# Attention of a Hymba-style step, regrouped: one narrow group of TensorE work per unit, with transposes two groups behind their scores

## The chip, the core and the metric

The kernel runs on one core of a Trainium2 chip. The metric is the device time of one execution in microseconds (us), the median of three runs. TensorE (PE) multiplies, VectorE (DVE), ScalarE (ACT) and GpSimd (POOL) do elementwise work, and SyncE (SP) issues the large loads.

## What is computed

One layer for 320 tokens (256 of a new stream, 64 of a running one), with `D_MODEL` 2048, 16 query heads and 2 key heads of 64, and an FFN of 8192. The reference, cut to what matters here:

```python
h = rmsnorm(x, ln_g); z = h @ w_in          # q 1024, k 128, v 128, u 1024, v 1024
q, k = rmsnorm(q, q_g), rmsnorm(k, k_g)     # per head
def sink_attention(q, k, v, bias, sinks):   # chunk of 64, own chunk and the 2 before it
    s = einsum(q, k) * HEAD_DIM ** -0.5 + bias
    m = maximum(max(s), sink)
    p = exp(s - m)
    return einsum(p / (sum(p) + exp(sink - m)), v)
a = gelu(zs); u, v = a[:1024], rmsnorm(a[1024:], g)
s_o = u * (w_s @ v + b_s)                   # 8 groups of channels, chunks of 128 positions
x = x + concat(rmsnorm(attn_o), rmsnorm(s_o)) @ w_out
y = x + square(relu(rmsnorm(x) @ w_up)) @ w_down
```

## The kernel before

Activations lie transposed: channels on partitions, 320 tokens along the free axis. Every dense product takes 256 columns of a weight at a time. A load (`w_raw`, 512 KB) brings 4 blocks of 128 rows; `halves` splits it into a high part (`w_hi`, ACT, L108) and the rest (`w_lo`, DVE, L109), and three matmuls high x high, high x low, low x high make up one product of float32 quality. Such a matmul (128x320 out, L133) is called a **wide** here, and one load a **step**: 24 wides. A product over 2048 rows has 4 steps, 96 wides. `w_hi` and `w_lo` have 3 buffers each, so a step's halves are written when the step three before it has been multiplied.

The wides run on in this order, counted from the first as W0: keys, values and q0 together up to W192, q1 to W288, q2 to W384, q3 to W480, four products for the SGU's `v` to W864, four for its `u` to W1248, `w_out` to W2016 (its attention half first), and then the FFN to W8160.

Everything else on PE is **narrow** float32 work between wides: `norm_q` (L311, sums of squares of q's heads), scores (`s_ps`, L385), transposes of the probabilities (L423), values (`o_ps`, L429), and for the SGU sums of rows (`rstd_rows`, L156), transposes (L485) and the spatial matmuls (L493). A **unit** of attention is a chunk of 64 queries with one key head; there are ten, `unit // 2` the chunk and `unit % 2` the head. Chunks 2 to 4 have 192 keys in two parts of 96, so two transposes each (`pt0`, `pt1`). Its softmax is spread over DVE (L394 to L404, L411, L412), ACT (L405, L409) and POOL (L413).

PSUM holds two accumulators (`acc`), one `s_ps`, and two buffers (`misc`) that all other narrow work shares. Each engine takes its instructions in the order of its own list. A scheduler lays these lists out when the kernel is built; `tc.issue_after(x)` puts what follows behind instruction x, and `between_pieces={n: ...}` places narrow work behind step n of a product. Attention (`attend`), the SGU's transposes and its spatial matmuls have no such place before; the scheduler spreads them among the wides of the `v` and the `u` products. `gelu2` (L452 to L460) reads a finished accumulator: `z` (DVE), a square (ACT), `gc` (DVE, then POOL), tanh (ACT), and the result (DVE).

Of the kernel before, what the change touches and what calls it, by code (L numbers as in the profile page):

```python
# [30 lines left out]
def hymba_step_kernel(ctx: ExitStack, tc: tile.TileContext, i, o):  # L31
# [63 lines left out]

    loads, between, steps, narrow = [], [], [], []

# [16 lines left out]

    def products(w, k0, nk, c0, ps, rh, rl, deep=None, between_pieces={}):

        wv = w.rearrange("(kt p) n -> p kt n", p=P)
        behind = None  # L120
        steps.clear()
        for a in range(0, nk, 4):
            raw = (deep or wp).tile([P, 4, 256], F32, name="w_raw", tag="w_raw")
            hi, lo = w_tiles()
            load(raw, wv[:, k0 + a:k0 + a + 4, c0:c0 + 256])
            high, low = halves(raw, hi, lo)
            tail = isinstance(ps, list) and a + 4 == nk
            for k, g in [(k, g) for g in range(2) for k in range(4)] if tail else [(k, g) for k in range(4) for g in range(2)]:
                kk = a + k
                for x, (w_, r_) in enumerate(((hi, rh), (hi, rl), (lo, rh))):  # L130
                    out = ps[g][:, 0:T] if isinstance(ps, list) else ps[:, g, 0:T]
                    with tc.issue_after(behind) if behind else nullcontext():
# [31 lines left out]
    def rstd(acc, mean, eps, out):  # L164
# [4 lines left out]
        nc.scalar.activation(out=hi, in_=acc, func=AF.Copy)  # L169
        nc.vector.tensor_tensor(out=lo, in0=acc, in1=hi.bitcast(F32), op=ALU.subtract)  # L170
        ps = misc()
# [83 lines left out]

    kzv = blk("kzv", [P, 1664])
    kz = kzv[:, 0:896].rearrange("p (h k) -> p h k", h=2)
# [69 lines left out]

    q1_ps = product(w_in, 0, KT, 256, xh, xl, between_pieces={0: lambda: rstd(ssq, mean_dm, EPS, rx)})

# [30 lines left out]
    q2_sq = evict_q(2, q2_ps)  # L360
    q3_ps = product(w_in, 0, KT, 768, xh, xl, between_pieces={0: lambda: norm_q(2, q2_sq)})
    norm_q(3, evict_q(3, q3_ps))


# [9 lines left out]

    def attend(unit):

        blk_, kv = unit // 2, unit % 2
        q0, k0, nk, b0, parts = blocks[blk_]
        js = slice(2 * kv, 2 * kv + 2)
        s_ps = ps_sc.tile([P, 2, 512], F32, name="s_ps", tag="s_ps")  # L380
        for j in range(2):
            a = 2 * (2 * kv + j)
            for p in range(2):
                hs = slice(p * HD, (p + 1) * HD)
                nc.tensor.matmul(out=s_ps[:, p, j * nk:(j + 1) * nk],  # L385
                                 lhsT=qT[hs, blk_, a:a + 2].rearrange("p a t -> p (a t)"),
                                 rhs=kz[hs, kv, k0:k0 + nk], start=True, stop=True)
        s = at.tile([P, 2, 2, 192], F32, name="s", tag="s", bufs=2)
        if nk < P:
# [17 lines left out]
        for p in range(2):  # L407
            for j in range(2):
# [5 lines left out]
                                in1=den[:, :, :, None].to_broadcast([P, 2, 2, nk]), op=ALU.mult)  # L414
        pts = []
        for x in range(len(parts)):
            pts.append(at.tile([P, 512], F32, name=f"pt{x}", tag=f"pt{x}", bufs=1))
        for x in reversed(range(len(parts))):
            n, c = parts[x][1], sum(n_ for _, n_ in parts[:x])
            pt_ps = misc()  # L420
            for p in range(2):
                for j in range(2):
                    nc.tensor.transpose(out=pt_ps[0:n, (2 * p + j) * P:(2 * p + j + 1) * P], in_=s[:, p, j, c:c + n],  # L423
                                        identity=ident)
            nc.vector.tensor_copy(out=pts[x][0:n], in_=pt_ps[0:n])
        o_ps = misc()
        for x, (pt, (v, n)) in enumerate(zip(pts, parts)):
            for p in range(2):
                nc.tensor.matmul(out=o_ps[p * HD:(p + 1) * HD, 0:256], lhsT=v[0:n, kv],  # L429
                                 rhs=pt[0:n, p * 256:(p + 1) * 256],  # L430
                                 start=(x == 0), stop=(x == len(parts) - 1))
# [11 lines left out]
    todo = list(range(10))
    after_q = [narrow[-1]]

    def attend_next(n):
        for _ in range(n):
            with tc.issue_after(after_q.pop()) if after_q else nullcontext():
                attend(todo.pop(0))

# [26 lines left out]
    rv = rstd_rows(acc_v, inv_1k, 4 * EPS)  # L477
    vnat = blk("vnat", [P, 2, 1024])
    vnat_s = at.tile([P, 1024], F32, name="vnat_s", bufs=1)
    nc.gpsimd.memset(vnat_s[HD:P], 0.0)  # L480
    for t, (t0, n) in enumerate(TT):
        for h in range(2):
            vps = misc()
            for a in range(4):
                nc.tensor.transpose(out=vps[0:n, a * P:(a + 1) * P], in_=gv[:, 4 * h + a, t0:t0 + n], identity=ident)  # L485
            dst = vnat[:, t] if t < 2 else vnat_s[0:HD]
            nc.scalar.activation(out=dst[:, h * 512:(h + 1) * 512], in_=vps[0:n], func=AF.Copy, scale=rv[0:n, t:t + 1])
    nc.gpsimd.dma_start(out=o["sgu_v"], in_=vnat_s[0:HD])
    for g in range(8):
        sp_ps = misc()  # L490
        cs = slice(g * P, (g + 1) * P)
        for b in range(2):
            nc.tensor.matmul(out=sp_ps[:, b * P:(b + 1) * P], lhsT=vnat[:, b, cs], rhs=wsT[:, g], start=True, stop=True)  # L493
        nc.tensor.matmul(out=sp_ps[:, 256:T], lhsT=vnat_s[:, cs], rhs=wsT[:, g, 0:HD], start=True, stop=True)
        nc.vector.tensor_tensor(out=gv[:, g, 0:256].rearrange("p (b i) -> p b i", b=2),
                                in0=sp_ps[:, 0:256].rearrange("p (b i) -> p b i", b=2),
                                in1=sgb[:, g, None, :].to_broadcast([P, 2, P]), op=ALU.add)
        nc.vector.tensor_tensor(out=gv[:, g, 256:T], in0=sp_ps[:, 256:T], in1=sgb[:, g, 0:HD], op=ALU.add)

    acc_s = sums("acc_s")  # L500
    rs_a, rm_a = [], rstd_b("rm_a")
    u_pieces = {3: {0: lambda: rs_a.append(rstd_rows(acc_a, inv_1k, EPS)), 2: lambda: spread(rs_a[0], rm_a)}}
    SH = SL = None
    for g in range(4):
        u_ps = product(w_in, 0, KT, 1280 + g * 256, xh, xl, between_pieces=u_pieces.get(g, {}))
        if g == 0:
            acc_a = sums_rows("acc_a")
            AH, AL = blk("AH", [P, 8, T], F32R), blk("AL", [P, 8, T], F32R)
            SH, SL = blk("SH", [P, 8, T], F32R), blk("SL", [P, 8, T], F32R)
        for x in range(2):  # L510
# [6 lines left out]
        gu = sm.tile([P, 2, T], F32, name="gu", tag="w2", bufs=4)  # L517
        gelu2(u_ps, gu)
        sp = gv[:, 2 * g:2 * g + 2]
        nc.vector.scalar_tensor_tensor(out=sp, in0=sp, scalar=0.5, in1=gu, op0=ALU.mult, op1=ALU.mult)  # L520
        for a in range(2 * g, 2 * g + 2):
            add_square(acc_s, gv[:, a], a == 0)
# [117 lines left out]
```

## Time and profile before

| what | value |
|---|---|
| median of 3 runs | 1257.11 us (1255.76 to 1257.68) |
| profiled execution, its time | 1254.9 us |
| its span in the trace | 1253.1 us |
| PE busy | 1245.4 us, 99% of the span |
| DVE, ACT, POOL busy | 658.8, 490.8, 97.0 us |
| granted clock of PE | 1.00 in the whole span |

The span is what the trace covers of the profiled execution, so 1.8 us of that execution lie outside it. The profiled execution is 2.2 us below the median. PE has some matmul in flight nearly all the time, and the 8160 wides are most of it. What a change of the narrow work does shows in where wides are interrupted and for how long.

### The profile page before, as it was taken

To read this page: it belongs to the slowest core of one execution; us is meant where nothing else is said; L and a number is where in the kernel's file an instruction comes from. 1 tells how busy PE (TensorE), PEld (TensorE's weight loads), DVE (VectorE), ACT (ScalarE), POOL (GpSimd) and SP (SyncE) were. 2 spreads that over 40 slices of the span, in tenths; PEclk is the share of its full clock that TensorE was granted. 3 is DMA by queue.
4 is the path that set the end of the run, shared out by engine and by line. 5 is a ranking of instruction groups with operands and counts; after the bars stand their busy time and mean duration, and the time that the engine had idled before them with its cause. 6 is when DMAs were issued, how large, how long until landed. Compare 5 with 4: busy or idle time off the path is not lost.

```text
span 1253.1 us, 20226 instructions
## 1 busy us (share of the span) xinstructions
PE 1245.4 (99%) x8519; PEld 1231.4 (98%) x8519; DVE 658.8 (53%) x767; ACT 490.8 (39%) x638; POOL 97.0 (8%) x97
## 2 busy tenths in 40 slices
PE   9999999999999999999999999999999999999998
PEld 8998899999999999999999999999999999999998
DVE  7848867776874443444444433444444444444443
ACT  7335556524544433323334333343333333443221
POOL 1223353301310000000000000000000000000000
PEclk9999999999999999999999999999999999999999
DMA  8743334644454444445454444445444444544550
GB/s 272 210 144 101 102 102 126 207 147 152 151 152 152 151 151 149 146 147 150 150 151 152 151 152 150 147 148 149 151 149 152 151 152 152 149 153 158 168 166 32
DMA packets 186555, 187.78 MB, mean 150 GB/s; under 512 B 6592, under 2 KB 185984, under 8 KB 186464
## 3 DMA queue, kind: packets, MB, share of 16 engines
q1 hardware_dynamic: 185824, 185.43, 47.7%
q8 instruction: 66, 1.08, 0.4%
q0 software_dynamic: 496, 1.03, 0.3%
q14 instruction: 25, 0.20, 0.0%
q10 hardware_dynamic: 144, 0.03, 0.0%
HBM read 182.91 MB, written 3.32 MB: 149 GB/s over the span
## 4 chain that ended last, share of the span: by engine, by line
PE 96%; DMA 2%; SPq 1%; ACT 0%; DVE 0%; issue 0%; ACTq 0%
PE acc L133 91%; PE misc L133 1%; DMA w_raw<-in_w_in 1%; PE misc L429 1%; PE s_ps L385 1%; DMA b_dram<-b_row 1%; PE misc L423 1%; SPq L103 1%; PE q_ps L237 0%; PE acc L237 0%; PE misc L311 0%; DMA w_first<-in_w_in 0%; ACT w_hi L108 0%; PE misc L493 0%; PE misc L485 0%; DVE w_lo L109 0%
## 5 line engine op out<-in xcount | busy, mean ns | idle before, releaser
L109 DVE TENSOR_TENSOR w_lo<-w_raw,w_hi 128x1024 fp32r<-128x1024 f32 x332 | 413.3, 1245 | 439.8 <-ACT w_hi L108 430.9
L108 ACT ACTIVATE w_hi<-w_raw 128x1024 fp32r<-128x1024 f32 x332 | 351.8, 1060 | 704.6 <-PE acc L133 675.0
L133 PE MATMUL acc<-H2H,w_hi 128*128 128x320 f32 x1024 | 316.4, 309 | 0.0
L133 PE MATMUL acc<-H2L,w_hi 128*128 128x320 f32 x1024 | 316.4, 309 | 0.0
L133 PE MATMUL acc<-H2H,w_lo 128*128 128x320 f32 x1024 | 316.4, 309 | 0.0
L133 PE MATMUL acc<-FH,w_hi 128*128 128x320 f32 x992 | 306.5, 309 | 0.0
L133 PE MATMUL acc<-FL,w_hi 128*128 128x320 f32 x992 | 306.5, 309 | 0.0
L133 PE MATMUL acc<-FH,w_lo 128*128 128x320 f32 x992 | 306.5, 309 | 0.0
L133 PEld LDWEIGHTS acc<-H2H,w_lo 128*128 128x128 f32 x1024 | 192.3, 188 | 0.0
L133 PEld LDWEIGHTS acc<-H2H,w_hi 128*128 128x128 f32 x1024 | 192.3, 188 | 0.0
L133 PEld LDWEIGHTS acc<-H2L,w_hi 128*128 128x128 f32 x1024 | 192.3, 188 | 0.0
L133 PEld LDWEIGHTS acc<-FH,w_hi 128*128 128x128 f32 x992 | 186.2, 188 | 0.0
L133 PEld LDWEIGHTS acc<-FL,w_hi 128*128 128x128 f32 x992 | 186.2, 188 | 0.0
L133 PEld LDWEIGHTS acc<-FH,w_lo 128*128 128x128 f32 x992 | 186.2, 188 | 0.0
L133 PE MATMUL acc<-XH,w_hi 128*128 128x320 f32 x352 | 110.5, 314 | 0.4 <-ACT ksq L334 0.4
L133 PE MATMUL acc<-XL,w_hi 128*128 128x320 f32 x352 | 110.2, 313 | 0.0
L133 PE MATMUL acc<-XH,w_lo 128*128 128x320 f32 x352 | 109.7, 312 | 0.0
L133 PEld LDWEIGHTS acc<-XH,w_hi 128*128 128x128 f32 x352 | 66.2, 188 | 2.2 <-issue 1.4
L133 PEld LDWEIGHTS acc<-XL,w_hi 128*128 128x128 f32 x352 | 66.2, 188 | 1.5 <-issue 1.4
L133 PEld LDWEIGHTS acc<-XH,w_lo 128*128 128x128 f32 x352 | 66.1, 188 | 1.0 <-issue 0.8
L557 DVE SCALAR_TENSOR_TENSOR tf<-acc,r 128x640 f32<-128x640 f32 x32 | 26.4, 825 | 41.9 <-PE acc L133 41.8
L571 DVE TENSOR_TENSOR xT<-xT,acc 128x640 f32<-128x640 f32 x31 | 25.5, 821 | 41.8 <-PE acc L133 41.8
(198 smaller groups left out, 1056.5 us busy)
## 6 DMA issues: line engine op xcount, KB each, us to landing
w_raw<-in_w_up SPq DMA_DIRECT2D x128, 512.0 KB
w_raw<-in_w_down SPq DMA_DIRECT2D x128, 512.0 KB
w_raw<-in_w_in SPq DMA_DIRECT2D x44, 512.0 KB
w_raw<-in_w_out SPq DMA_DIRECT2D x32, 512.0 KB
w_first<-in_w_in SPq DMA_DIRECT2D x15, 256.0 KB
out_yT<-xT SPq DMA_DIRECT2D x7, 320.0 KB
xT<-in_xT SPq DMA_DIRECT2D x8, 160.0 KB
xT<-in_xT SPq DMA_DIRECT2D x4, 320.0 KB
```

What stands on the lines that cost most here:

```text
L103: loads.append(nc.sync.dma_start(out=o_, in_=i_))
L108: return (pin(nc.scalar.activation(out=hi, in_=raw, func=AF.Copy)).ins, pin(nc.vector.tensor_tensor(out=lo, in0=raw, in1=hi.bitcast(F32), ...
L109: pin(nc.vector.tensor_tensor(out=lo, in0=raw, in1=hi.bitcast(F32), op=ALU.subtract)).ins)
L133: mm = nc.tensor.matmul(out=out, lhsT=w_[:, k, g * P:(g + 1) * P], rhs=r_(kk), start=(kk == 0 and x == 0), stop=(kk == nk - 1 and x == 2))
L385: nc.tensor.matmul(out=s_ps[:, p, j * nk:(j + 1) * nk], lhsT=qT[hs, blk_, a:a + 2].rearrange("p a t -> p (a t)"), rhs=kz[hs, kv, k0:k0 + n ...
L423: nc.tensor.transpose(out=pt_ps[0:n, (2 * p + j) * P:(2 * p + j + 1) * P], in_=s[:, p, j, c:c + n], identity=ident)
L429: nc.tensor.matmul(out=o_ps[p * HD:(p + 1) * HD, 0:256], lhsT=v[0:n, kv], rhs=pt[0:n, p * 256:(p + 1) * 256], start=(x == 0), stop=(x == l ...
L557: nc.vector.scalar_tensor_tensor(out=t, in0=ps[:, :, 0:T], scalar=0.0, in1=r2[:, None, :].to_broadcast([P, 2, T]), op0=ALU.max, op1=ALU.mult)
L571: nc.vector.tensor_tensor(out=xT[:, a:a + n], in0=xT[:, a:a + n], in1=p, op=ALU.add)
```

## The change

- Units are taken head by head (all chunks of key head 0, then of 1). `attend(i)` is now one group: the values of unit i-3, the scores of unit i, the transposes of unit i-2. Group i stands at W432 + 48 i, that is behind steps 1 and 3 of q3 and of the `v` products, and the last three groups in the first two `u` products.
- Probabilities `s` have three buffers. The transposed probabilities lie at the ends of `kzv` and of a tile `room` that also holds `vnat`.
- `norm_q(2)` moves from W408 to W432, `norm_q(3)` from W512 to W528. The SGU's transposes stand at W984, W1008 and W1032, its spatial matmuls by twos from W1056 on.
- A pin (`behind`) at the end of a product now holds for the wides of the next one (`carry`).
- x's norm: DVE takes the split of `acc` (L170) ahead of `w_lo` of q1's third step.
- `SH` is written one `u` product later, and its rest `SL` (8 DVE passes) moves into the attention half of `w_out`.

```diff
@@ products @@
-        behind = None
+        behind = carry.pop() if carry else None
...
-            high, low = halves(raw, hi, lo)
+            with tc.issue_after(halves_behind[a // 4]()) if a // 4 in halves_behind else nullcontext():
+                high, low = halves(raw, hi, lo)
...
                     behind = narrow[-1]
+                if a + 4 == nk:
+                    carry.append(behind)
@@ rstd, q1 @@
-        nc.vector.tensor_tensor(out=lo, in0=acc, in1=hi.bitcast(F32), op=ALU.subtract)
+        rests.append(nc.vector.tensor_tensor(out=lo, in0=acc, in1=hi.bitcast(F32), op=ALU.subtract).ins)
...
-    q1_ps = product(w_in, 0, KT, 256, xh, xl, between_pieces={0: lambda: rstd(ssq, mean_dm, EPS, rx)})
+    q1_ps = product(w_in, 0, KT, 256, xh, xl, between_pieces={0: lambda: rstd(ssq, mean_dm, EPS, rx)},
+                    halves_behind={2: lambda: rests[-1]})
@@ attention @@
-    q3_ps = product(w_in, 0, KT, 768, xh, xl, between_pieces={0: lambda: norm_q(2, q2_sq)})
-    norm_q(3, evict_q(3, q3_ps))
...
+    units = [(b, kv) for kv in range(2) for b in range(5)]
+    probs, turned = {}, {}
+    room = blk("vnat", [P, 2560])
+    vnat = room[:, 0:2048].rearrange("p (t c) -> p t c", t=2)
+    pts = [kzv[:, 1664:2176], room[:, 2048:2560]]
...
-        s = at.tile([P, 2, 2, 192], F32, name="s", tag="s", bufs=2)
+        s = at.tile([P, 2, 2, 192], F32, name="s", tag="s", bufs=3)
...
+    def attend(i):
+
+        for stage, u in ((values_of, i - 3), (scores, i), (turn, i - 2)):
+            if 0 <= u < 10:
+                with tc.issue_after(narrow[-1]):
+                    stage(u)
+
+    q3_ps = product(w_in, 0, KT, 768, xh, xl,
+                    between_pieces={1: lambda: (norm_q(2, q2_sq), attend(0)), 3: lambda: attend(1)})
+    q3_sq = evict_q(3, q3_ps)
@@ SGU @@
-        attend_next((4, 3, 3, 0)[g])
-        v_ps = product(w_in, 0, KT, 2304 + g * 256, xh, xl)
+        v_ps = product(w_in, 0, KT, 2304 + g * 256, xh, xl, between_pieces={
+            1: lambda: (norm_q(3, q3_sq) if g == 0 else None, attend(2 * g + 2)), 3: lambda: attend(2 * g + 3)})
...
+        0: {1: lambda: attend(10), 3: last_values},
+        1: {0: lambda: by_rows((0, 0), (1, 0)), 1: lambda: (attend(12), by_rows((2, 0), (0, 1))),
+            2: lambda: by_rows((1, 1), (2, 1)), 3: lambda: spatial(0, 1)},
+        2: {0: lambda: spatial(2, 3), 1: lambda: spatial(4, 5), 2: lambda: spatial(6, 7)},
...
-            split(gv[:, a], g_os[:, a:a + 1], SH[:, a], SL[:, a])
...
+            if half == 0:
+                with tc.issue_after(steps[0][1]):
+                    nc.vector.scalar_tensor_tensor(out=SL[:, g], in0=gv[:, g], scalar=g_os[:, g:g + 1],
+                                                   in1=SH[:, g].bitcast(F32), op0=ALU.mult, op1=ALU.subtract)
```

PE's list, before, in the fourth `v` product (`acc_1807`): the values of one unit, a transpose of the next and the scores of a later one, then wides, then the other transpose.

```order
L133 MATMUL acc_1807<-XH_117,w_lo_1840 128x320
L429 MATMUL misc_1389<-pt0_1375,kzv_438 64x256 x2
L429 MATMUL misc_1389<-pt1_1376,kzv_438 64x256 x2
L423 MATMUL misc_1560<-ident_88,s_1537 96x128 x4
L385 MATMUL s_ps_1624<-kzv_438,qT_119 128x192 x4
L133 MATMUL acc_1807<-XH_117,w_hi_1839 128x320
...
L133 MATMUL acc_1807<-XL_118,w_hi_1839 128x320
L423 MATMUL misc_1566<-ident_88,s_1537 96x128 x4
L133 MATMUL acc_1807<-XH_117,w_lo_1840 128x320
```

PE's list of the change at W672, group 5: values of unit 2, scores of unit 5, and both transposes of unit 3.

```order
L134 MATMUL acc_1229<-XH_117,w_lo_1364 128x320
L447 MATMUL misc_1392<-kzv_438 64x256 x2
L447 MATMUL misc_1392<-vnat_827,kzv_438 64x256 x2
L392 MATMUL s_ps_1398<-kzv_438,qT_119 128x64 x4
L435 MATMUL misc_1425<-ident_88,s_1188 96x128 x4
L435 MATMUL misc_1431<-ident_88,s_1188 96x128 x4
L134 MATMUL acc_1453<-XH_117,w_hi_1455 128x320
```

The eleven wides between the two transposes are gone from that place, and the group needs three `misc` tiles in a row (values, transpose, transpose) where two buffers exist.

DVE's list, before, around the transposes of the ninth unit (`s_1583`): its copies `pt1`, `pt0` stand a `w_lo` behind the softmax of the last unit (`s_1629`).

```order
L402 TENSOR_SCALAR nm_1637<-m_1634 128x4
L404 TENSOR_TENSOR es_1639<-sinks_440,m_1634 128x4
L411 TENSOR_TENSOR den_1642<-den_1642,es_1639 128x4
L412 RECIPROCAL den_1642<-den_1642 128x4
L109 TENSOR_TENSOR w_lo_2076<-w_raw_2074,w_hi_2075 128x1024
L454 TENSOR_TENSOR z_1928<-acc_1807,rx_471 128x640
L425 COPY pt1_1605<-misc_1606 96x512
L109 TENSOR_TENSOR w_lo_2106<-w_raw_2104,w_hi_2105 128x1024
L425 COPY pt0_1604<-misc_1612 96x512
```

DVE's list of the change between groups 9 (W864) and 10 (W912): the end of unit 9's softmax (`den_1851`), then the copies of unit 8's two transposes (`misc_1959`, `misc_1965`).

```order
L481 SCALAR_TENSOR_TENSOR gv_1014<-gc_1873,z_1871 128x640
L408 TENSOR_TENSOR m_1843<-m_1843,sinks_440 128x4
L109 TENSOR_TENSOR w_lo_2003<-w_raw_2001,w_hi_2002 128x1024
L410 TENSOR_SCALAR nm_1846<-m_1843 128x4
L412 TENSOR_TENSOR es_1848<-sinks_440,m_1843 128x4
L205 SCALAR_TENSOR_TENSOR AL_2060<-ao_120,cols_82,AH_2059 128x320
L419 TENSOR_TENSOR den_1851<-den_1851,es_1848 128x4
L437 COPY kzv_438<-misc_1959 96x512
L420 RECIPROCAL den_1851<-den_1851 128x4
L109 TENSOR_TENSOR w_lo_2084<-w_raw_2082,w_hi_2083 128x1024
L437 COPY vnat_827<-misc_1965 96x512
```

The whole softmax of unit 9 now stands between the gelu of the last `v` product and these copies: the copy of `misc_1959` stands directly behind `den_1851`. The two copies are those that free `misc` for what PE does in group 10.

ACT's list, before, around the square that `norm_q(2)` reads (`qsq_825`): it stands behind `w_hi` of q3's last step.

```order
L108 ACTIVATE w_hi_898<-w_raw_897 128x1024
L108 ACTIVATE w_hi_928<-w_raw_927 128x1024
L305 ACTIVATE qsq_825<-qT_119 128x640
L108 ACTIVATE w_hi_1124<-w_raw_1123 128x1024
L108 ACTIVATE w_hi_1154<-w_raw_1153 128x1024
```

ACT's list of the change at the same square: one more `w_hi` stands ahead of it, that of the first `v` product's first step.

```order
L108 ACTIVATE w_hi_956<-w_raw_955 128x1024
L108 ACTIVATE w_hi_1019<-w_raw_1018 128x1024
L308 ACTIVATE qsq_825<-qT_119 128x640
L417 ACTIVATE s_903,den_917<-s_903,nm_912 128x64
L413 ACTIVATE es_914<-es_914 128x4
```

The square moved one step later, as `norm_q(2)` did.

## Rows read from the trace of the kernel before

**Rows 1.** The page: busy time of each engine, share of the span, instructions.

```profile
PE 1245.4 (99%) x8519; PEld 1231.4 (98%) x8519; DVE 658.8 (53%) x767; ACT 490.8 (39%) x638; POOL 97.0 (8%) x97
```

**Rows 2.** The chain that ended last: start us, us, what (x instructions).

```profile
358.08 877.65 PE acc L133 x5984
```

**Rows 3.** The same chain, 133 to 142 us.

```profile
133.39 1.01 PE misc L429 x8
134.40 0.57 PE misc L423 x4
134.98 0.85 PE s_ps L385 x8
135.83 2.54 PE acc L133 x16
138.36 0.44 PE misc L423 x4
138.80 3.66 PE acc L133 x25
```

**Rows 4.** The same chain, 70 to 74 us.

```profile
70.92 1.06 ACT w_hi L108
71.98 0.69 ACT qsq L305
72.72 1.28 PE misc L311 x10
```

**Rows 5.** PE's timeline, 38 to 39 us: start, us, line, instruction, [idle before].

```profile
38.04 0.31 PE L172 MATMUL misc<-n_hl,mean_dm 128*128 128x320 f32 x1
38.54 0.42 PE L173 MATMUL misc<-n_hl,mean_dm 128*128 128x320 f32 x1 [0.19 <-DVE n_hl L170]
38.79 0.31 PE L133 MATMUL acc<-XH,w_hi 128*128 128x320 f32 x1
```

**Rows 6.** The chain that ended last, 39 to 50 us.

```profile
39.79 6.79 DMA w_raw<-in_w_in
47.78 1.22 DVE w_lo L109
49.00 0.41 DVE zk L331
49.95 3.75 PE acc L133 x24
```

**Rows 7.** Groups by line: count | busy us, mean ns of one | idle before, releaser.

```profile
L394 DVE SCALAR_TENSOR_TENSOR s<-s_ps,rq,bias 128x192 f32<-128x192 f32 (+2 forms) x40 | 12.4, 367 | 1.3 <-PE s_ps L385 1.3
L402 DVE TENSOR_SCALAR nm<-m 128x4 f32<-128x4 f32 x10 | 3.2, 320 | 0.2
L409 ACT ACTIVATE s<-s,nm 128x192 f32<-128x192 f32 (+2 forms) x40 | 16.4, 411 | 8.4 <-DVE es L404 4.4 <-DVE nm L402 3.9
L425 DVE COPY pt<-misc 96x512 f32<-96x512 f32 (+1 forms) x16 | 10.8, 682 | 3.3 <-PE misc L423 3.3
L432 ACT ACTIVATE ao<-misc 128x256 f32<-128x256 f32 x10 | 3.8, 376 | 8.3 <-PE misc L429 8.2
L454 DVE TENSOR_TENSOR z<-acc,rx 128x640 f32<-128x640 f32 x8 | 6.6, 821 | 3.7 <-PE acc L133 3.4
L457 DVE TENSOR_SCALAR gc<-gc 128x640 f32<-128x640 f32 x8 | 5.1, 641 | 0.9 <-ACT gc L456 0.9
L458 POOL TENSOR_TENSOR gc<-gc,z 128x640 f32<-128x640 f32 x8 | 13.7, 1706 | 23.3 <-DVE gc L457 23.3
L459 ACT ACTIVATE gc<-gc 128x640 f32<-128x640 f32 x8 | 5.9, 735 | 4.0 <-POOL gc L458 3.8
```

**Rows 8.** Timelines of POOL and of DVE, 127 to 129 us.

```profile
127.49 1.47 POOL L413 TENSOR_TENSOR s<-s,den 128x768 f32<-128x768 f32 x1 [2.60 <-DVE den L412]
...
127.57 1.73 DVE L457 TENSOR_SCALAR gc<-gc 128x640 f32<-128x640 f32 x1 [0.25 <-ACT gc L456]
```

**Rows 9.** Busy time by stretch: PE, PEld, DVE, ACT, POOL, then clock, DMA share, GB/s.

```profile
260.00:280.00 20.00, 20.00 (x138) 20.00 (x137) 15.61 (x23) 6.35 (x6) 0.00 (x0) 1.00 0.50 159
```

More of the change, by code (lines that the diff above doesn't have):

```diff
@@ L93, in hymba_step_kernel @@
     nc.vector.memset(hone[HD:P, 1:2], 1.0)
-    loads, between, steps, narrow = [], [], [], []
+    loads, between, rests, steps, narrow, carry = [], [], [], [], [], []
     def load(out, in_):
@@ L113, in w_tiles, with products @@
                 wp.tile([P, 4, 256], F32R, name="w_lo", tag="w_lo", bufs=3))
-    def products(w, k0, nk, c0, ps, rh, rl, deep=None, between_pieces={}):
+    def products(w, k0, nk, c0, ps, rh, rl, deep=None, between_pieces={}, halves_behind={}):
         wv = w.rearrange("(kt p) n -> p kt n", p=P)
-        behind = None
+        behind = carry.pop() if carry else None
         steps.clear()
@@ L254, in hymba_step_kernel @@
     nc.sync.dma_start(out=kn[:, 256:384], in_=i["ckT"])
-    kzv = blk("kzv", [P, 1664])
+    kzv = blk("kzv", [P, 2176])
     kz = kzv[:, 0:896].rearrange("p (h k) -> p h k", h=2)
@@ L373, in hymba_step_kernel, with scores @@
     sinks_pj = sinks.rearrange("x (p j) -> x p j", p=2)
-    def attend(unit):
-        blk_, kv = unit // 2, unit % 2
+    units = [(b, kv) for kv in range(2) for b in range(5)]
[3 more added lines that the diff above has]
+    pts = [kzv[:, 1664:2176], room[:, 2048:2560]]
+    def scores(u):
+        blk_, kv = units[u]
         q0, k0, nk, b0, parts = blocks[blk_]
@@ L384, in attend @@
                 hs = slice(p * HD, (p + 1) * HD)
-                nc.tensor.matmul(out=s_ps[:, p, j * nk:(j + 1) * nk],
-                                 lhsT=qT[hs, blk_, a:a + 2].rearrange("p a t -> p (a t)"),
-                                 rhs=kz[hs, kv, k0:k0 + nk], start=True, stop=True)
-        s = at.tile([P, 2, 2, 192], F32, name="s", tag="s", bufs=2)
+                mm = nc.tensor.matmul(out=s_ps[:, p, j * nk:(j + 1) * nk],
+                                      lhsT=qT[hs, blk_, a:a + 2].rearrange("p a t -> p (a t)"),
+                                      rhs=kz[hs, kv, k0:k0 + nk], start=True, stop=True)
+        narrow.append(mm.ins)
+        s = at.tile([P, 2, 2, 192], F32, name="s", tag="s", bufs=3)
         if nk < P:
@@ L414, in attend, with turn @@
                                 in1=den[:, :, :, None].to_broadcast([P, 2, 2, nk]), op=ALU.mult)
[L415 to L419, printed above, removed]
+        probs[u] = s
+    def turn(u):
+        s, parts = probs.pop(u), blocks[units[u][0]][4]
+        turned[u] = []
+        for x, (v, n) in enumerate(parts):
+            c = sum(n_ for _, n_ in parts[:x])
+            pt = pts[x]
             pt_ps = misc()
@@ L422, in attend, with values_of @@
                 for j in range(2):
-                    nc.tensor.transpose(out=pt_ps[0:n, (2 * p + j) * P:(2 * p + j + 1) * P], in_=s[:, p, j, c:c + n],
-                                        identity=ident)
-            nc.vector.tensor_copy(out=pts[x][0:n], in_=pt_ps[0:n])
+                    mm = nc.tensor.transpose(out=pt_ps[0:n, (2 * p + j) * P:(2 * p + j + 1) * P],
+                                             in_=s[:, p, j, c:c + n], identity=ident)
+            nc.vector.tensor_copy(out=pt[0:n], in_=pt_ps[0:n])
+            turned[u].append((pt, v, n))
+        narrow.append(mm.ins)
+    def values_of(u):
+        blk_, kv = units[u]
+        q0, parts = blocks[blk_][0], turned.pop(u)
         o_ps = misc()
-        for x, (pt, (v, n)) in enumerate(zip(pts, parts)):
+        for x, (pt, v, n) in enumerate(parts):
             for p in range(2):
-                nc.tensor.matmul(out=o_ps[p * HD:(p + 1) * HD, 0:256], lhsT=v[0:n, kv],
-                                 rhs=pt[0:n, p * 256:(p + 1) * 256],
-                                 start=(x == 0), stop=(x == len(parts) - 1))
+                mm = nc.tensor.matmul(out=o_ps[p * HD:(p + 1) * HD, 0:256], lhsT=v[0:n, kv],
+                                      rhs=pt[0:n, p * 256:(p + 1) * 256], start=(x == 0), stop=(x == len(parts) - 1))
+        narrow.append(mm.ins)
         nc.scalar.activation(out=ao[:, 4 * kv:4 * kv + 4, q0:q0 + 64],
                              in_=o_ps[:, 0:256].rearrange("p (a q) -> p a q", a=4), func=AF.Copy)
+    def attend(i):
[6 more added lines that the diff above has]
+    q3_sq = evict_q(3, q3_ps)
     def add_square(acc, src, first):
@@ L441, in add_square @@
             nc.gpsimd.tensor_tensor(out=acc[:, 0:T], in0=acc[:, 0:T], in1=sq, op=ALU.add)
[L443 to L449, printed above, removed]
     def gelu2(ps, out):
@@ L476, in hymba_step_kernel, with by_rows @@
     nc.gpsimd.memset(wsT[HD:P, :, 0:HD], 0.0)
-    rv = rstd_rows(acc_v, inv_1k, 4 * EPS)
-    vnat = blk("vnat", [P, 2, 1024])
     vnat_s = at.tile([P, 1024], F32, name="vnat_s", bufs=1)
     nc.gpsimd.memset(vnat_s[HD:P], 0.0)
-    for t, (t0, n) in enumerate(TT):
-        for h in range(2):
-            vps = misc()
+    rv = []
+    def by_rows(*ths):
+        for t, h in ths:
+            (t0, n), vps = TT[t], misc()
             for a in range(4):
-                nc.tensor.transpose(out=vps[0:n, a * P:(a + 1) * P], in_=gv[:, 4 * h + a, t0:t0 + n], identity=ident)
+                mm = nc.tensor.transpose(out=vps[0:n, a * P:(a + 1) * P], in_=gv[:, 4 * h + a, t0:t0 + n],
+                                         identity=ident)
@@ L486, in hymba_step_kernel @@
             dst = vnat[:, t] if t < 2 else vnat_s[0:HD]
[L487 to L498, printed above, removed]
+            nc.scalar.activation(out=dst[:, h * 512:(h + 1) * 512], in_=vps[0:n], func=AF.Copy,
+                                 scale=rv[0][0:n, t:t + 1])
@@ new lines, in by_rows, with spatial @@
+        narrow.append(mm.ins)
+        if ths[-1] == (2, 1):
+            nc.gpsimd.dma_start(out=o["sgu_v"], in_=vnat_s[0:HD])
+    def spatial(*gs):
+        for g in gs:
+            sp_ps = misc()
+            cs = slice(g * P, (g + 1) * P)
+            for b in range(2):
+                nc.tensor.matmul(out=sp_ps[:, b * P:(b + 1) * P], lhsT=vnat[:, b, cs], rhs=wsT[:, g], start=True,
+                                 stop=True)
+            mm = nc.tensor.matmul(out=sp_ps[:, 256:T], lhsT=vnat_s[:, cs], rhs=wsT[:, g, 0:HD], start=True, stop=True)
+            nc.vector.tensor_tensor(out=gv[:, g, 0:256].rearrange("p (b i) -> p b i", b=2),
+                                    in0=sp_ps[:, 0:256].rearrange("p (b i) -> p b i", b=2),
+                                    in1=sgb[:, g, None, :].to_broadcast([P, 2, P]), op=ALU.add)
+            nc.vector.tensor_tensor(out=gv[:, g, 256:T], in0=sp_ps[:, 256:T], in1=sgb[:, g, 0:HD], op=ALU.add)
+        narrow.append(mm.ins)
@@ L500, in hymba_step_kernel, with last_values @@
+    def last_values():
+        attend(11)
+        with tc.issue_after(narrow[-1]):
+            rv.append(rstd_rows(acc_v, inv_1k, 4 * EPS))
     acc_s = sums("acc_s")
     rs_a, rm_a = [], rstd_b("rm_a")
-    u_pieces = {3: {0: lambda: rs_a.append(rstd_rows(acc_a, inv_1k, EPS)), 2: lambda: spread(rs_a[0], rm_a)}}
-    SH = SL = None
+    u_pieces = {
+        0: {1: lambda: attend(10), 3: last_values},
+        1: {0: lambda: by_rows((0, 0), (1, 0)), 1: lambda: (attend(12), by_rows((2, 0), (0, 1))),
+            2: lambda: by_rows((1, 1), (2, 1)), 3: lambda: spatial(0, 1)},
+        2: {0: lambda: spatial(2, 3), 1: lambda: spatial(4, 5), 2: lambda: spatial(6, 7)},
+        3: {0: lambda: rs_a.append(rstd_rows(acc_a, inv_1k, EPS)), 2: lambda: spread(rs_a[0], rm_a)}}
@@ L504, in hymba_step_kernel, with gate @@
+    gus = {}
+    def gate(g):
+        sp = gv[:, 2 * g:2 * g + 2]
+        nc.vector.scalar_tensor_tensor(out=sp, in0=sp, scalar=0.5, in1=gus[g], op0=ALU.mult, op1=ALU.mult)
+        for a in range(2 * g, 2 * g + 2):
+            add_square(acc_s, gv[:, a], a == 0)
+            nc.scalar.activation(out=SH[:, a], in_=gv[:, a], func=AF.Copy, scale=g_os[:, a:a + 1])
     for g in range(4):
@@ L508, in hymba_step_kernel @@
             AH, AL = blk("AH", [P, 8, T], F32R), blk("AL", [P, 8, T], F32R)
-            SH, SL = blk("SH", [P, 8, T], F32R), blk("SL", [P, 8, T], F32R)
         for x in range(2):
@@ L516, in hymba_step_kernel @@
                 add_square(acc_a, ao[:, a], a == 0)
[L517 to L522, printed above, removed]
-            split(gv[:, a], g_os[:, a:a + 1], SH[:, a], SL[:, a])
+        if g:
+            if g == 1:
+                SH = blk("SH", [P, 8, T], F32R)
+            gate(g - 1)
+        gus[g] = sm.tile([P, 2, T], F32, name="gu", tag="w2", bufs=4)
+        gelu2(u_ps, gus[g])
+    gate(3)
     phase1.close()
     wf = ctx.enter_context(tc.tile_pool(name="wf", bufs=7))
+    SL = blk("SL", [P, 8, T], F32R)
     H2H, H2L = big("H2H"), big("H2L")
```

## The prediction

> **What bounds the kernel now.** I read the page first. PE is busy for 99% of the span [rows 1], so only what PE issues, or waits for, can move the time. The chain that ended last gives the price of a wide: 5984 of them in a row take 877.65 us, .1467 each [rows 2]. Times 8160 that is 1196.8 us, and 1253.1 − 1196.8 = 56.3 us of the span go to the start, the end, narrow work and waits. The chain between the wides is then the view for a change of narrow work.
>
> One stretch of it shows all prices [rows 3]. Eight records of values (L429; a float32 instruction leaves two) take 1.01 us, eight of scores .85, four of transposes .44. What matters here is what a change of kind costs. The 16 wides behind scores take 2.54 us where 16 × .1467 = 2.35: the entry costs **.19**. The 25 wides behind transposes take 3.66, which is 25 × .1467: that entry is free. Transposes behind values take .57 in place of .44: .13. Scores behind transposes show nothing extra.
>
> **Part 1: fewer, larger groups.** The narrow instructions are the same, so only entries change. I counted them in the two orders between W408 and W1176.
> - Before: 40 runs of wides. 16 of them follow values or scores: 16 × .19 = 3.0. Three transposes follow values: .4. Four more entries of the first kind (scores of two units cut by wides, the sums of rows, the first spatial matmuls): .8. Sum 4.2.
> - After: 20 runs. Two follow scores alone: .4. Two transposes follow values: .26. Eight follow scores directly; no row of before shows that, it lies between 0 and .19, and I take .14 (as behind values): 1.1. Seven scores follow values, unseen too, between 0 (as behind transposes) and .19; I take .05: .35. The sums of rows and the spatial matmuls keep .35. Sum 2.5.
> - So 1.7 us are saved; with the unseen entries at 0 it would be 3.2, with all at .19 about .3 (15 × .19 in place of 1.45).
> - The values' transposes (L323) wait a little in q2 before; the pin that holds them moves with the new order, worth .1.
>
> **Part 2: norm_q(2) later.** The chain shows a wait of 1.8 us: PE's wides hand over at 70.92 to ACT's `w_hi`, 1.06, then comes `qsq`, .69, and the sums start at 72.72 [rows 4]. ACT's list has `qsq` behind the `w_hi` of q3's last step, whose buffer is free only when PE is through with the step in front of the sums. With the change the sums go one step later, but so does `qsq`: it now stands behind the next `w_hi`, whose buffer is freed by exactly the step in front of the sums' new place. I expect the same 1.8 at W432, so **0**. If ACT reached `qsq` in time it would be −1.8.
>
> **Part 3: x's norm.** PE's two matmuls take from 38.04 to 38.79, .75 where two wides take .29 [rows 5]; the wait for DVE is at most .46. With L170 ahead of `w_lo` it goes. But PE then stands at W288: it resumes at 49.95 behind `zk` (49.00), behind `w_lo` (47.78), behind a load that landed at 39.79 + 6.79 = 46.58 [rows 6]. The load, not PE, sets that end, so PE waits there for what it saved: **0**, at most −.46.
>
> **Part 4: SL, SH, the moved SGU work.** SL's eight DVE passes go to the attention half of `w_out`; there DVE is busy 15.61 of 20 us [rows 9], so each pass of about .8 (as L454 [rows 7]) has over 4 us free per 20 and nothing on PE reads SL before W1632. 0; without that room it would be 6. SH a product later, a third `s`, the sums of squares: ACT and DVE work off the path, 0.
>
> **Part 5: three misc tiles in a group, with two buffers.** This is the price of the larger group. In a group with two transposes PE needs a buffer for the values, one for the first transpose and one for the second. The second waits until ACT has evicted the values (`ao`, .38) or DVE has copied the first transpose (.68) [rows 7]. Before, wides filled that time. Where in ACT's and DVE's lists these evictions stand decides:
> - W624: `ao` stands behind the four exps of a softmax (1.64), behind tanh and two squares. About .35.
> - W672: a product ends there, and `ao` stands behind `z` (.82) and ACT's square (.73, as tanh). .82 + .73 + .38 = 1.93, hand-overs .2; PE would be ready after values 1.01, scores of 64 keys (.5, an estimate from .85 for 192) and .44: about .2.
> - W912 (group 10): the second transpose takes the buffer of the first, so it waits for its copy, at least .68 + .1 of hand-over. The copy stands behind `den` of unit 9, which waits for its exps. Counted from the end of the last `v` product: `z` .82, a `w_lo` 1.25, four score passes 4 × .37, `gc` .64 on DVE, 1.71 on POOL, tanh .74, `w_hi` 1.06, `w_lo` 1.22, two small passes .32 each, exps 1.64, `den` .2, the copy .68: 11.8 with hand-overs 12.3 [rows 4, 6, 7]. PE is ready at about 2.4 (group 9) + 48 × .1467 + 1.58 (values and a transpose) = 11.0. Wait 1.3. DVE and POOL also hinder each other: while POOL's pass ran from 127.49 for 1.47, DVE's `gc` took 1.73 in place of .64 [rows 7, 8]. In this chain `AL` (two inputs in SBUF) stands beside POOL's pass, worth up to 1.0 more: 2.3. I take 1.6, nearer the first since only one pass meets POOL's.
> - W960 (group 11): `ao` behind `w_hi` (1.06) and ACT's square: PE ready at 1.58, `ao` done at 2.1 to 2.4, .6 to .8; then the sums of rows need the first transpose's copy, behind a `w_lo`: .25. About 1.0.
> - W1008: two transposes of `gv` behind the last values: .2.
>
> Sum .35 + .2 + 1.6 + 1.0 + .2 = 3.35; the bounds are 1.7 (.78 at W912, .5 at W960, none elsewhere but .4) and 5 (2.3 to 3 at W912, 1.3 at W960, .7 together elsewhere).
>
> The Trainium skill ("SBUF — State Buffer", section "Who interferes with whom") says that DVE and GpSimd share one pair of ports and that the holder locks the other out. The trace agrees, with 1.73 us for the pass above. By that page each such meeting costs a whole POOL pass, which would put the wait at W912 at its upper end.
>
> **The sum.** −1.7 − .1 + 0 + 0 + 0 + 3.35 = +1.5 us. The profiled execution takes 1254.9, so 1256.4 for a profile of the change; the median of the runs stands 2.2 above the profiled execution, so **1258.6** for the median. A measurement of this kernel can tell about .2%, 2.5 us, from no change.
>
> **Rivals.**
> - **A (likeliest, .58): saving and new waits about cancel**, as summed: −.5 to +2.5, so 1256.6 to 1259.6.
> - **B (.12): the groups pay nothing new.** PE finds its misc buffers free, because the scheduler's lists of ACT and DVE run earlier on the chip than I make them (for it: the slack of ACT, 39% busy [rows 1]; against it: W912 needs the copy whatever comes earlier). Then −1.8 + .8 = −1.0; with `qsq` in time −2.8 and with entries between narrow kinds at 0 up to −4.3: 1254.3 to 1252.8. It decides if the second transposes of the groups wait less than .3 each.
> - **C (.22): the softmax of unit 9 is late.** One mechanism, at W912: POOL's `gc` and `AL` collide, tanh comes late, `w_hi` and with it `w_lo`, `nm` and the exps. Each us of lateness is a us of PE. From a wait of 2.7 on the sum passes +2.5; at 4 it is 1256.9 + 2.0 + 2.0 = 1261.
> - **D (.03): the change does in full what its two edits of order say.** By my reading x's norm and `norm_q(2)` don't do what they are written for and give 0; if both gave what they remove, −.46 − 1.8 = −2.3, the sum becomes −.8: 1256.3, still no change. Against it stands ACT's list, and the landing at 46.58 [rows 6].
> - **E (.05): entries are free,** and what looked like one was work. Then nothing is saved by larger groups and the sum is −.1 + 3.35 = +3.3: 1260.4. Against it stand the .19 behind scores [rows 3].
>
> The Trainium skill ("TensorE: Matmul & The Clock Gate", section "Step-by-step: what each phase is for") says PE pulls a weight load ahead of matmuls in flight, so that the next weights load while a matmul runs. By that rule entries would be free and E holds. The trace shows it only for wides behind transposes (0), not behind scores (.19).
>
> **How the numbers follow.** No change holds A, D and the low end of C (.01): .62. Slower by over .2% (above 1259.6) holds the rest of C, and E: .26. Faster by over .2% (below 1254.6) holds B: .12. The range leaves out half of B and the end of C: 1255.2 to 1261.2; the likeliest one's own range is 1256.6 to 1259.6.
>
> **What would show it.** In the profile after: wides in runs of 24 between W432 and W1176, at 3.5 us behind transposes; a chain with `w_hi` and `qsq` of 1.8 us near 76 us; PE's second matmul of x's norm without a wait, but still wides from about 49.95; PE idle before the second transposes, most at W912 (about 145 us; releaser DVE's copy, or `den` and exps) and W960. Wrong would be: no idle there (B), a wait at W912 over 2.7 (C), scores and values that are followed by transposes at over .19 per entry, or a stall of `w_lo` in `w_out` that comes from SL.

## The result, and the profile after

The changed kernel takes 1260.81 us, the median of 15 runs (1257.21 to 1265.33), against 1257.27 for the kernel before (15 runs, 1255.59 to 1259.94): a ratio of 1.0033, 95% interval 1.0023 to 1.0044. It is slower, by more than the .2% that I took as the bound. The profiled execution took 1259.32 us, with a span of 1256.6.

The page of the changed kernel, its busy times. PE is as busy as in [rows 1], DVE 8 us less.

```profile
PE 1246.9 (99%) x8519; PEld 1234.4 (98%) x8519; DVE 650.7 (52%) x767; ACT 489.6 (39%) x638; POOL 100.5 (8%) x97
```

The answer of the trace on the core: span, and mean granted clock of PE. Before it was 1.00.

```profile
core 0: 1256.6 us, clock 0.998
```

So first the place where the clock was lost. Busy time by stretch of the changed kernel: PE, PEld, DVE, ACT, POOL, then the granted clock, DMA share and GB/s.

```profile
78.00:79.00 1.00, 1.00 (x9) 0.91 (x8) 0.17 (x1) 0.00 (x0) 0.56 (x1) 0.53 0.84 245
79.00:80.00 1.00, 1.00 (x6) 0.97 (x4) 0.86 (x4) 0.00 (x0) 1.00 (x1) 0.50 1.08 359
...
81.00:82.00 1.00, 1.00 (x7) 1.00 (x7) 0.00 (x0) 1.00 (x8) 0.00 (x0) 0.76 0.24 82
```

From 78 to 82 us the granted clock is .50 to .76 (the row left out has .50), so PE ran at 1.2 of its 2.4 GHz for more than three microseconds. What stood ahead of that is in the chain of the changed kernel at W432 (start us, us, what):

```profile
70.70 3.54 PE acc L134 x24
74.24 0.02 issue
74.26 0.84 DVE qT L303
75.10 1.02 ACT w_hi L108
76.12 0.64 ACT qsq L308
76.75 0.04 issue
76.80 1.28 PE misc L314 x10
78.07 1.03 PE s_ps L392 x8
79.10 8.33 PE acc L134 x48
87.43 0.65 PE s_ps L392 x8
88.07 7.23 PE acc L134 x48
```

The chain waits from 74.24, when q2 is complete, to 76.80: 2.56 us, where [rows 4] have 1.8. PE itself still runs 4 wides of q3 in that time; its timeline gives the stall, 1.99 us here and (second row) 1.69 before:

```profile
76.80 1.28 PE L314 MATMUL misc<-hone,qsq 128*128 128x2 f32 x10 [1.99 <-ACT qsq L308]
72.72 1.28 PE L311 MATMUL misc<-hone,qsq 128*128 128x2 f32 x10 [1.69 <-ACT qsq L305]
```

What fills the wait is in ACT's and DVE's timelines, here the changed kernel's and then, behind the dots, those of the kernel before:

```profile
74.11 2.00 ACT L108 ACTIVATE w_hi<-w_raw 128x1024 fp32r<-128x1024 f32 x2 [5.50 <-PE acc L134]
76.02 0.72 ACT L308 ACTIVATE qsq<-qT 128x640 f32<-128x640 f32 x1
74.26 0.82 DVE L303 TENSOR_TENSOR qT<-acc,rx 128x640 f32<-128x640 f32 x1 [3.23 <-PE acc L134]
...
70.92 1.06 ACT L108 ACTIVATE w_hi<-w_raw 128x1024 fp32r<-128x1024 f32 x1 [2.75 <-PE acc L133]
71.93 0.74 ACT L305 ACTIVATE qsq<-qT 128x640 f32<-128x640 f32 x1
71.07 0.82 DVE L300 TENSOR_TENSOR qT<-acc,rx 128x640 f32<-128x640 f32 x1 [1.64 <-PE acc L133]
```

`qT`, the eviction of q2, stands in both waits, beside a `w_hi`; the chain of the change names it, but ACT's first `w_hi` lasts as long. New is a second `w_hi` behind it: the first starts only as q2's last step ends, 7 us after q2 should have been through. Behind the stall the scores take 1.03 (.59 at full clock) and 48 wides 8.33 (7.23 where the next 48 run), 1.5 us more.

The second place is group 10 (W912). PE's timeline, then DVE's and POOL's:

```profile
171.89 0.64 PE L435 MATMUL misc<-ident,s 128*96 128x128 f32 x4
174.67 0.64 PE L435 MATMUL misc<-ident,s 128*96 128x128 f32 x4 [2.14 <-DVE kzv L437]
...
170.22 0.85 DVE L410 TENSOR_SCALAR nm<-m 128x4 f32<-128x4 f32 x1
...
173.17 0.85 DVE L419 TENSOR_TENSOR den<-den,es 128x4 f32<-128x4 f32 x1 [1.27 <-POOL gv L496]
173.94 0.68 DVE L437 COPY kzv<-misc 96x512 f32<-96x512 f32 x1
...
170.00 1.04 POOL L470 TENSOR_TENSOR acc_v<-acc_v,sq 128x320 f32<-128x320 f32 x1 [2.67 <-ACT sq L469]
...
173.14 0.85 POOL L470 TENSOR_TENSOR acc_v<-acc_v,sq 128x320 f32<-128x320 f32 x1
```

Four transposes take .44, so PE waited from 172.33 to 174.67, 2.3 us (2.14 idle by the timeline), for the copy of the group's first transpose, which stands behind `den` of unit 9. The last of its exps started at 172.54; `den`, four values per partition, began at 173.17 and took .85 beside POOL's second pass on `acc_v`, and `nm` ahead of the exps had taken .85 beside the first.

The groups without a wait look as they were meant to. Group 5 (W672) of the changed kernel in the chain:

```profile
123.56 1.01 PE misc L447 x8
124.57 0.59 PE s_ps L392 x8
125.17 1.01 PE misc L435 x8
126.17 7.04 PE acc L134 x48
```

Scores start .00 behind values, the eight transposes take 1.01 (two times .44 and .13 behind scores), and the 48 wides take exactly 48 × .1467 = 7.04.

### The profile page after: what moved, and what is told of

Its sections match the earlier page's. It is cut to its first block, busy times and chain, and to the rows that moved or that the text cites. A ratio compares the mean times of both kernels' runs of the same rounds, so it can differ in the third digit from the quotient of the medians.

```text
span 1256.6 us, 20213 instructions
## 1 busy us (share of the span) xinstructions
PE 1246.9 (99%) x8519; PEld 1234.4 (98%) x8519; DVE 650.7 (52%) x767; ACT 489.6 (39%) x638; POOL 100.5 (8%) x97
## 3 DMA queue, kind: packets, MB, share of 16 engines
q0 software_dynamic: 496, 1.03, 0.3%
## 4 chain that ended last, share of the span: by engine, by line
PE 98%; ACT 1%; DVE 1%; POOL 0%; DMA 0%; issue 0%; SPq 0%; DVEq 0%; POOLq 0%
PE acc L134 91%; PE acc L240 1%; PE q_ps L240 1%; PE misc L134 1%; PE s_ps L392 1%; PE misc L435 0%; PE misc L447 0%; ACT w_hi L108 0%; PE misc L314 0%; DMA w_first<-in_w_in 0%; PE misc L521 0%; PE misc L507 0%; POOL gv L496 0%; POOL gc L479 0%; ACT s L417 0%
```

## The experiments

Each run is compared with the kernel before as measured beside it (medians 1257.27, 1257.11 and 1257.38); times against the change are differences of medians.

Two theories stood against each other. Theory B is the prediction's: the new waits for `misc` tiles in groups 10 and 11 eat the saving. Theory A: the loss sits at W432. PE's list shows why q2 is late there; these are its rows in the changed kernel (`acc_636` is q2, `acc_828` is q3):

```
L134 MATMUL acc_828<-XL_118,w_hi_860 128x320
L326 MATMUL misc_790<-ident_88,kvx_436 96x128
L134 MATMUL acc_636<-XH_117,w_hi_794 128x320
...
L134 MATMUL acc_636<-XH_117,w_lo_795 128x320
L134 MATMUL acc_828<-XH_117,w_lo_861 128x320
L134 MATMUL acc_828<-XH_117,w_hi_860 128x320
L134 MATMUL acc_828<-XL_118,w_hi_860 128x320
L134 MATMUL acc_828<-XH_117,w_lo_861 128x320
L314 MATMUL misc_889<-hone_113,qsq_825 128x2 x5
```

q2's last 24 wides are pinned behind the fifth transpose of the values (`narrow[-1]`), q3's are not. So 44 wides of q3 stand ahead of the fifth transpose and pass them (24 in the kernel before), and q2 is complete only 4 wides ahead of the sums that need its square.

**q2_ahead** takes the change and lets only the first two transposes pin q2's last step:

```diff
-            narrow.append(nc.tensor.transpose(out=vps[0:n, 0:P], in_=vT[:, t0:t0 + n], identity=ident).ins)
+            tr = nc.tensor.transpose(out=vps[0:n, 0:P], in_=vT[:, t0:t0 + n], identity=ident).ins
+            if x < 2:
+                narrow.append(tr)
```

> The changed kernel, with q3's wides kept from passing q2's last step (only the first two transposes of the values pin it). Theory A (the loss sits at W432: q2's last step ran 44 wides late, so its eviction, a w_hi and qsq all fell into one stall of 2.6 us, and PE's clock fell behind it): the stall at W432 is under .4, the granted clock stays at 1.00 from 70 to 90 us, and the time falls by about 4 us against the changed kernel's 1260.8, to about 1256.8. Theory B (the prediction's: the stall at W432 is as before, the loss is the waits for misc tiles in groups 10 and 11): at most 1.8 us are saved, 1259.0 or more, and the waits at W912 and W960 stand as they were (2.3 and about .6).

Measured: 1255.64 us (12 runs), ratio to the kernel before .9987 (.9977 to .9997). Its chain at W432:

```profile
69.95 4.11 PE acc L134 x28
74.06 1.01 PE misc L314 x10
75.07 0.59 PE s_ps L394 x8
75.66 7.23 PE acc L134 x48
```

No stall is left there, 48 wides take 7.23, and the time fell by 5.2 us where A said 4. The wait at W912 stayed (the second transposes start at 170.13, behind `den` and its copy), and this time the clock fell there. The same view of q2_ahead as above:

```profile
170.00:180.00 10.00, 9.87 (x60) 9.44 (x60) 4.18 (x7) 2.74 (x5) 2.27 (x1) 0.83 0.23 71
```

**turns_apart** takes the change and puts the second transposes of units 8 and 9 a step later:

```diff
-        0: {1: lambda: attend(10), 3: last_values},
-        1: {0: lambda: by_rows((0, 0), (1, 0)), 1: lambda: (attend(12), by_rows((2, 0), (0, 1))),
-            2: lambda: by_rows((1, 1), (2, 1)), 3: lambda: spatial(0, 1)},
-        2: {0: lambda: spatial(2, 3), 1: lambda: spatial(4, 5), 2: lambda: spatial(6, 7)},
+        0: {1: lambda: attend(10, (0,)), 2: lambda: second(8), 3: last_values},
+        1: {0: lambda: (second(9), by_rows((0, 0))), 1: lambda: (attend(12), by_rows((1, 0))),
+            2: lambda: by_rows((2, 0), (0, 1)), 3: lambda: by_rows((1, 1), (2, 1))},
+        2: {0: lambda: spatial(0, 1), 1: lambda: spatial(2, 3), 2: lambda: spatial(4, 5), 3: lambda: spatial(6, 7)},
```

In this kernel and in q2_and_turns the first gate of the SGU runs ahead of the spatial matmuls that it should read; the work is the same in amount.

> The changed kernel, with the second transposes of units 8 and 9 taken out of groups 10 and 11 and put one step later, the SGU's transposes and spatial matmuls a step later where they have to be. Theory B: the idle time at W912 (2.3) and before W984 (.6) goes, about 2.7 us: 1258.1. Theory A has nothing against that, but its larger loss stays: the stall of 2.6 us at W432 and the low clock behind it. If the waits of groups 10 and 11 were only a symptom of PE being early (softmax late anyway), PE would wait at the next place instead and less than 1 us would be saved: 1260 or more.

Measured: 1256.13 us (12 runs), ratio .9988 (.9978 to .9998): 4.7 us less than the change, where B said 2.7. The waits of group 10 are gone. The stall at W432 stayed, as expected, and was dearer than in the profile above: its chain

```profile
75.81 1.30 PE misc L314 x10
77.11 1.05 PE s_ps L392 x8
78.16 9.77 PE acc L134 x48
```

with 48 wides in 9.77, 2.5 us over 7.23, at a clock of .50 from 78 to 82.

**q2_and_turns** has both edits. 

> Both edits together. Theories A and B add up: 4 + 2.7 = 6.7 us less than the changed kernel, about 1254.1, which is 3 us less than the kernel before (ratio .9975). If A alone is right: 1256.8; if B alone: 1258.

Measured: 1251.64 us (6 runs), ratio .9960 (.9944 to .9975), granted clock .999 or 1.00 in every execution. The two losses add up, and there is more in them (9.2 us) than the two theories said (4 and 2.7).

**fill_432** asks what that surplus is. It takes the change and gives PE something to do while it waits at W432:

```diff
+    def filler(n):
+        f_ps = ps_sc.tile([P, 2, 512], F32, name="f_ps", tag="s_ps")
+        for _ in range(n):
+            mm = nc.tensor.matmul(out=f_ps[:, 0, 0:T], lhsT=mean_dm, rhs=XH[:, 0], start=True, stop=True)
+        narrow.append(mm.ins)
...
-                    between_pieces={1: lambda: (norm_q(2, q2_sq), attend(0)), 3: lambda: attend(1)})
+                    between_pieces={1: lambda: (filler(16), norm_q_behind(), attend(0)), 3: lambda: attend(1)})
```

> The changed kernel with 16 matmuls of 128x320 put on PE ahead of norm_q(2) at W432, whose result nothing reads: the wait for qsq stays as long (2.6 us), but PE is busy in it. If the low clock behind the stall comes from PE standing idle, the granted clock stays at 1.00 from 74 to 90 us, the 48 wides behind take 7.0 instead of 8.3, and the time falls by about 1.7 us, to 1259.1. If the clock fell for another reason, the 48 wides take 8.3 as before and the time stays at 1260.8 or rises.

Measured: 1258.22 us (12 runs), ratio 1.0008 (.9999 to 1.0017). The chain:

```profile
73.90 2.35 PE f_ps L463 x16
76.25 1.01 PE misc L314 x10
77.26 0.59 PE s_ps L392 x8
77.85 7.24 PE acc L134 x48
```

The lists of all engines are those of the change, but for the 16 matmuls. They take 2.35, a little longer than PE stood, so nothing is shorter; the wait is only busy. The wides behind it run at full clock, and 2.6 us came back. As in q2_ahead, the clock then fell behind the wait at W912 (.83 from 170 to 180).

**fill_both** adds the same filler between the two transposes of group 10. (It also pins the two transposes of each group one behind the other; the lists are again those of the change, but for the fillers.)

```diff
+            if u == 8 and x == 1:
+                filler(16)
```

> The changed kernel with 16 matmuls of 128x320 that nothing reads at each of its two longest waits: ahead of norm_q(2) at W432, and between the two transposes of group 10 at W912. The waits stay as long, PE is busy in them. If the changed kernel's loss against the kernel before is mostly the low clock behind these two waits, the granted clock is .998 or more in every execution (what the start takes is left), and the time falls by 3 to 4 us from 1260.8 to about 1257.3, the kernel before's. If the waits themselves are the loss, the time stays above 1259.5.

Measured: 1256.25 us (11 runs), ratio 1.0003 (.9993 to 1.0014), granted clock 1.00 in all eleven executions. Nothing was made shorter, and 4.6 us came back (3.8 by the two ratios, of the 4.1 that the change had lost). Nearly all of the loss against the kernel before is the clock behind the change's two longest waits.

**before_q2** has q2_ahead's edit on the kernel before. 

> The kernel before, with nothing changed but the pin of q2's last step (behind the first two transposes of the values, so that no wide of q3 passes it). Theory A: the wait of 1.8 us for qsq goes, and with it the lower clock of some executions: 1.8 to 2.3 us, 1255. The rest of what q2_and_turns gained (about 3.5) is then the groups' and the norm's. If the groups themselves gain nothing, this kernel is as fast as q2_and_turns, 1251.6.

Measured: 1253.57 us (7 runs), ratio .9971 (.9960 to .9981), clock 1.00 in all. 3.8 us for a pin: the 1.8 of [rows 4] are gone (PE's sums start at 70.84 behind the wides that end there), and so are the low clocks that the kernel before shows in some executions.

**norm_only** has the new order of x's norm on the kernel before. 

> The kernel before, with x's norm alone in the new order (DVE's rest of the sums ahead of w_lo of q1's third step). The prediction: PE gains .46 at W216 and gives it back at W288, 0 in all: 1257.1. The rival, from the profiles of the changed kernels (which resumed .3 to .6 earlier at W288 too): .5 to .7 us is kept, 1256.5, with wides of the next product starting that much earlier.

Measured: 1257.79 us (12 runs), ratio 1.0005 (.9996 to 1.0014): no change. The two matmuls of x's norm take .29 in place of .75 and PE reaches W216 .46 earlier, counted from W24; the wait is gone in all profiles with this edit. What W288 makes of it differs from one execution to the next, from .6 us earlier (the change) to 1.24 later (q2_and_turns_2), since a load that lands at its own time ends that wait. Its profile happens to show what becomes of the kernel before in an unlucky execution; the chain at the old place of norm_q(2):

```profile
72.24 1.06 ACT w_hi L108
73.30 0.69 ACT qsq L306
...
74.03 1.71 PE misc L312 x10
75.75 14.36 PE acc L134 x79
```

It is the wait of [rows 4], 1.8 us (1.69 idle), but the sums behind it take 1.71 in place of 1.28, and 79 wides 14.36 in place of 11.59.

**q2_and_turns_2** is q2_and_turns with the spatial matmuls left where the change had put them, so that the gates read them:

```diff
-        1: {0: lambda: (second(9), by_rows((0, 0))), 1: lambda: (attend(12), by_rows((1, 0))),
-            2: lambda: by_rows((2, 0), (0, 1)), 3: lambda: by_rows((1, 1), (2, 1))},
-        2: {0: lambda: spatial(0, 1), 1: lambda: spatial(2, 3), 2: lambda: spatial(4, 5), 3: lambda: spatial(6, 7)},
+        1: {0: lambda: (second(9), by_rows((0, 0))), 1: lambda: (attend(12), by_rows((1, 0), (2, 0))),
+            2: lambda: by_rows((0, 1), (1, 1)), 3: lambda: (spatial(0, 1), by_rows((2, 1)))},
+        2: {0: lambda: spatial(2, 3), 1: lambda: spatial(4, 5), 2: lambda: spatial(6, 7)},
```

> The two edits of the run q2_and_turns, with the spatial matmuls left at the places that the change gave them, ahead of the gates that read them. Theory A and B together: as that run, 1251.6, ratio to the kernel before .996, granted clock .999 to 1.00 in every execution. If that run owed its time to the SGU's other places, 1 us or more is lost again: 1252.7 or more.

Measured: 1252.52 us (5 runs, 1251.40 to 1252.92), ratio .9962 (.9949 to .9974), clock 1.00 in all. It beats both kernels. Its chain shows what the third tile costs at W1056, where the last by-rows transpose waits for a `misc` buffer:

```profile
198.33 0.41 DVE gv L529
198.74 0.14 DVE gv L532
...
199.02 0.60 PE misc L512 x4
```

## Why the prediction failed, step by step

To compare the kernels where they differ, take from each trace the start of wide W384 and of W1248 and subtract 864 × .1467 = 126.7: what is left is narrow work and waits.

| kernel | W384 to W1248 | left | of it slow clock |
|---|---|---|---|
| before | 168.0 | 41.3 | 0 |
| changed | 171.3 | 44.6 | about 1.5 |
| fill_both | 169.9 | 43.2 | 0 |
| before_q2 | 166.1 | 39.4 | 0 |
| q2_and_turns_2 | 165.0 | 38.3 | 0 |

- **The sum failed, and the step is that it prices a wait by its length.** I took the granted clock of 1.00 in one profiled execution of before for a property of the kernel and had no term for it. Without the slow clock the changed kernel is worth about what I summed. Between W384 and W1248, where the sum's terms lie, fill_both takes 1.8 us more than the kernel before, where I had +1.5; from the first wide to the last it is .96, since W288 ends earlier in this execution. Among executions with a clock of 1.00 the spans agree: median 1254.5 for the eleven of fill_both (1254.0 to 1257.5) against 1253.4 for eleven of the kernel before (1252.2 to 1254.1). The clock made the rest. Over all executions the mean granted clock of the changed kernel is .994 to .998, median .996; that of before, in the 54 executions beside the experiments, .997 to 1.00, median .999. Each .001 of 1257 us is 1.26 us, so the medians are 3.8 us apart by the clock alone (to ± 1.3, since it is given in thousandths); the measured medians are 3.5 apart. A single reading is less safe: one execution of norm_only has .947 and took 1257.97 us.
- **That 1260.8 is close to rival C's 1261 is luck:** C gave it for a wait of 4 at W912, and that wait was 2.3.
- **Part 2, norm_q(2), failed in size.** I forecast the same wait at W432; PE stood 1.99 in place of 1.69, and the chain's wait was 2.56 in place of 1.8. I read ACT's list, which has one more `w_hi` ahead of `qsq`, and not PE's, which has q2's last step behind 44 wides of q3. So two `w_hi` (2.00) fell into the wait in place of one (1.06). Even the 1.8 of before was not ACT's order alone: without q3's 24 wides ahead of q2's last step it goes too (before_q2).
- **Part 1, the groups, held.** Forecast 1.7 saved. q2_and_turns_2 against before_q2 has 39.4 − 38.3 = 1.1 less left, and about .9 us of waits for `misc` is still in it (.5 before the sums of rows, .1 at W1008, .25 at W1056, the PE work of each group taken off): about 2. The medians, 1252.52 and 1253.57, differ by that 1.1, but their intervals overlap. The unseen entries came out as .13 to .15 for transposes behind scores (taken: .14), 0 for scores behind values (taken: .05). Wides behind scores still pay .19 (7.23 for 48, above), so rival E is out. By the Trainium skill ("TensorE: Matmul & The Clock Gate", section "Step-by-step: what each phase is for") the next weights load beside a running matmul. That holds here behind transposes and not behind scores: at 97.48 the first weights begin to load together with the last transpose, at 88.00 they begin .20 behind the start of the last score.
- **Part 3, x's norm, held:** .46 at W216 and no change in the time (norm_only).
- **Part 4 held:** from W1248 to W2016 both kernels take 112.93 us.
- **Part 5, three tiles on two buffers, held in mechanism and nearly in size.** W624 .2 (forecast .35), W672 0 (.2), W912 2.3 (1.6), W960 1.0 (1.0), W1008 .1 (.2): 3.6 against 3.35. (The chain that I added up for W912 makes 12.1 and not 11.8, and W912 lies at 171 us and not near 145.) At W912 DVE was hindered by POOL, as rival C has it, below C's threshold of 2.7 and at other instructions than `gc` and `AL`: `nm` and `den` took .85 each beside POOL's passes on `acc_v` (means of before .32 and .22). The Trainium skill ("SBUF — State Buffer", section "Who interferes with whom") says that DVE and GpSimd lock each other out of a shared pair of ports; the rows agree, with .85 for `den`.
- **B and D are out:** the waits are there, and of the two edits of order one gives 0 and the other made its wait longer, by .3.

The profiled execution of the change also starts 1.56 us later (W24, counted from W0) at a low clock of its first wides: up to 9.8 us they start .27 apart, as behind W432, though the view of the stretches prints 1.00 there. norm_only's has the same (1.68), the others have up to .5, so this is no property of the change. In fill_both the eleven executions lie in two groups, 1255.7 to 1256.3 and 1257.7 to 1259.3, all at a clock of 1.00. What tells them apart stays open; the load at W288 is a candidate, and so is the clock of the start, which the mean granted clock doesn't show.

## What to carry to other kernels

A stall of PE in the middle of dense work has two prices: its length, and what the clock does behind it, which one profile may not show; read the granted clock of all executions. A stall of about 2 us that the clock fell behind cost 3.5 us and more here. When narrow work is pinned by `narrow[-1]`, look in PE's own list at what the scheduler lets pass the pinned wides: a product whose last step is pinned and whose successor is not will be overtaken, and everything that reads it is late. Before larger groups of narrow work are made, count their PSUM tiles against the buffers: a group that needs one more than there are waits for an eviction that wides used to hide.

## What was unexpected in the hardware

PE's clock went to half behind stalls as short as 1.7 to 2.1 us (idle times of PE's timeline) inside a stream that was otherwise dense, and not each time. Behind 1.99 us at W432 it fell in the changed kernel (1.5 us lost) and in turns_apart (2.5 lost in the wides and .5 in the scores); behind 2.14 us at W912 it did not fall in the profiled execution of the changed kernel, but did in those of q2_ahead and fill_432; behind 1.69 us at W408 it stayed at 1.00 in the kernel before and fell in norm_only (2.8 lost in the wides). With PE kept busy by matmuls that nothing reads, it was 1.00 in eleven executions of eleven.
